# Sums of squares inside the next tile's matmuls, and a final norm with two tiles scaled ahead

## The chip, the cores and the metric

The kernel runs on one core of one Trainium2 chip, as one launch. The metric is the device time of that launch in microseconds (us), from the first to the last work of the core. The engines are called by their names in the profile: PE (TensorE, matrix products), DVE (VectorE), ACT (ScalarE), POOL (GpSimd) and SP (SyncE, which issues the DMAs here). Each engine has its own list of instructions, whose order the program fixes.

## The reference, cut to what matters

A trunk of two layers over 512 tokens of 1024 channels in fp32. Each layer has a token mixer (layer 0 a Fourier mixer, layer 1 a bidirectional retention) and a SwiGLU channel mixer. Ahead of each stands an RMS norm with a scale and a shift made from a conditioning vector; the mixer's output, times a gate, is added to x. One more norm with scale and shift ends it.

```
def rmsnorm(x, g):
    return x * lax.rsqrt(jnp.mean(x * x, axis=-1, keepdims=True) + EPS) * g

for i in range(DEPTH):
    sh1, sc1, g1, sh2, sc2, g2 = jnp.split(c_act @ w_ada[i] + b_ada[i], 6, axis=-1)
    h = modulate(rmsnorm(x, norm_mix_g[i]), sh1, sc1)
    m = fourier_mixer(h, w) if i % 2 == 0 else retention_mixer(h, ...)
    x = x + g1[:, None, :] * m
    h = modulate(rmsnorm(x, norm_ffn_g[i]), sh2, sc2)
    x = x + g2[:, None, :] * swiglu(h, w_ffn_in[i], w_ffn_out[i])
shf, scf = jnp.split(c_act @ w_ada_final + b_ada_final, 2, axis=-1)
return modulate(rmsnorm(x, final_norm_g), shf, scf)
```

So a norm needs, for each token, a sum over all 1024 channels of the x that the product ahead of it has just finished.

## The kernel before

**Layout.** x lies with channels on the partitions: 8 tiles of 128 channels by 512 tokens, kept in pairs as x[0] to x[3] (x_92 to x_95 in the program of the first layer, x_8944 to x_8950 of the second). An fp32 product is three matmuls of rounded parts (`mm3`, lines 209 to 211): high by high, high by low, low by high. `split` makes the parts: ACT casts the high part (L203), DVE takes the difference (L204).

**The four boundaries.** Four times an output projection is followed by a norm: Fourier to channel mixer 0 (the first boundary, some 75 to 130 us into the run), channel mixer 0 to retention (the second, about 447 to 500), retention to channel mixer 1 (the third, about 862 to 912), and channel mixer 1 to the final norm (the fourth, from 1203 to the end). The last piece of that projection is `out_product_last` (L599). It goes over token half t = 0, 1 (256 tokens each) and in each over the eight channel tiles j. Tile (t, j) is 12 matmuls (24 in the first boundary, which does four tiles there), then `add_gated` (L570, one DVE instruction, L571), which adds the gated product to x.

**The sums.** `Norm.sums(t, j)` (L420) turns the tile's two 128-token blocks onto the token partitions by two PE transposes (L426, called a pair here) into PSUM; they read what `add_gated` has written. After j = 3, 6 and 7 ACT squares what has been gathered and sums it (L432), and DVE scales and adds the sums (L434, L436). `SUMS = 2` says how far the sums lag: those of a tile are issued two tiles of matmuls after it, and `last_sums` (L634) does the last two.

**The rates and the modulation.** `rsqrt_steps` (L213) makes the reciprocal roots by a chain of small DVE steps (L220, L228, L231), `rate` (L445) spreads them over the partitions by two more transposes (L451), and `half` then forms the normed tiles: `modulated` (L473) is one DVE instruction (L474: x times the scale column times the rates in PSUM) and one or two ACT instructions which add the shift (L478 for the rounded high part, L479 for the fp32 one). In the second and third boundary `Quarters.half` lets DVE take the low parts by a subtraction (L508) over two tiles at a time, so an L508 needs an L478 and an L479 of both. The modulation of token half 0 (`spread(0, 0)`, `spread(0, 1)`) is emitted right after tile (1, 3), so it lies beside the products of tiles (1, 4) to (1, 7). The products that use it follow: L924 in retention and in the first channel mixer, L878 in the second one. At the end `Final.half` (L561) modulates and writes each pair of tiles with one DMA of 256 KB (L566).

**What sets the order.** The program is written as a list of steps, and a scheduler orders each engine's instructions by priority when the program is built; sums, gated adds and modulations are marked urgent (`tc.high_priority`). After that the order on each engine is fixed. Around the boundaries DVE and ACT also prepare weights: the casts and subtractions of lines 203 and 204, and sums of weight blocks (L339), all 128x1024.

Of the kernel before, what the change touches and what calls it, by code (L numbers as in the profile page):

```python
# [14 lines left out]
ALU = mybir.AluOpType  # L15
# [17 lines left out]
MASK_W = 896  # L33
LOOK = 4
LOADS = 4
SUMS = 2
URGENT = 500
PLAIN = ("00", "01", "10", "11")

# [116 lines left out]
def trunk(ctx, tc, A, where, out):  # L156
    nc = tc.nc
# [15 lines left out]
    def ps():  # L173
        return psum.tile([P, 512], F32, name="ps")

    def t2k():
        return tmp.tile([P, 512], F32, name="t2k")
# [8 lines left out]
    def tok(m):  # L186
        return slice(m * P, (m + 1) * P)

    def half(n):
        return slice(n * 512, (n + 1) * 512)  # L190
# [4 lines left out]
    def k2(t):  # L195
        return t.rearrange("p (k c) -> p k c", k=2)
# [9 lines left out]
    def mm3(o, a, b, first, last, **kw):  # L206

        (ah, al), (bh, bl) = a, b
        nc.tensor.matmul(o, ah, bh, start=first, stop=False, **kw)  # L209
        nc.tensor.matmul(o, ah, bl, start=False, stop=False, **kw)  # L210
        nc.tensor.matmul(o, al, bh, start=False, stop=last, **kw)  # L211
# [48 lines left out]
    def xt(j):  # L260

        return x[j // 2][:, half(j % 2)]
# [10 lines left out]
    def add(fn, *needs):  # L273
        program.append((needs, fn))
# [3 lines left out]
    loads, ready, mods, opening, wide, plain, homes = {}, {}, {}, set(), set(), set(), {}  # L278
# [40 lines left out]
    def use_next():  # L319
        step = steps[state["step"]]  # L320
        state["step"] += 1
        state["piece"] += len(pieces_of(step))
        issue(state["piece"] + LOADS)
        if step[0] == "ada":
            conditioning(step, loads.pop(step))
        elif len(step) == 5:
            ready[step] = combined(step)
        else:
            h, low = (k2(t) for t in high_low(loads.pop(step)))
            ready[step] = [(h[:, k, :], low[:, k, :]) for k in range(2)]  # L330
# [34 lines left out]
    def settle(key, q=ND - 1):  # L365
        if key not in shares:
            q = ND - 1
        last = at["ada", *key, q]
        while state["step"] <= last:
            use_next()  # L370
        for name, it in closing:
            if name[:2] == key and name[2] <= q:
                for _ in it:
                    pass
# [34 lines left out]
    def part(t):  # L409
        return slice(t * 256, (t + 1) * 256)  # L410
# [70 lines left out]
    class Quarters(Norm):  # L481
# [9 lines left out]
        def half(self, t, k):  # L491
            q = t4k()
            halves = [half(n) for n in range(2)]

            def held_of(tag):
# [61 lines left out]
    class Final(Norm):  # L557
        def start(self):
            pass

        def half(self, t, k):  # L561
            for j in range(4 * k, 4 * k + 4, 2):
                y = t2k()
                for i in range(2):
                    self.modulated(t, j + i, y[:, part(i)])
                nc.sync.dma_start(out=out[j * P : (j + 2) * P, part(t)].rearrange("(k p) t -> p k t", p=P), in_=k2(y))  # L566
                yield


    def add_gated(key, j, sl, o):  # L570
        nc.vector.scalar_tensor_tensor(  # L571
            out=xt(j)[:, sl], in0=o, scalar=mods[key][:, j : j + 1], in1=xt(j)[:, sl], op0=ALU.mult, op1=ALU.add
        )
# [25 lines left out]
    def out_product_last(a, names, key, following, ns=range(2)):  # L599

        w, squared = {}, []

        def act(t, n, *pieces):
            if t == 0:
                w[n] = [b for piece in pieces for b in piece]
                if n == ns[0]:
                    settle(key)
                    made["norm"] = following()
            nxt = made["norm"]
            if ns[0] == n:  # L610
                squared.extend((t, j) for j in range(4 * n))
            for c in range(4):
                j = 4 * n + c
                o = ps()[:, 0:256]
                for k, b in enumerate(w[n]):
                    first, last = k == 0, k == len(w[n]) - 1
                    b, m = [p[:, tok(c)] for p in b], [p[:, part(t)] for p in a(k)]
                    mm3(o, b, m, first, last)
                with tc.high_priority(offset=URGENT):
                    add_gated(key, j, part(t), o)  # L620
                squared.append((t, j))
                while len(squared) > SUMS:
                    nxt.sums(*squared.pop(0))
                if (t, j) == (1, 3 if ns[0] == 0 else 6):
                    nxt.rate(0)
                    nxt.spread(0, 0)
                    if ns[0] == 0:
                        nxt.spread(0, 1)

        for t in range(2):  # L630
            for n in ns:
                add(lambda *p, t=t, n=n: act(t, n, *p), *(names[n] if t == 0 else ()))

    def last_sums():  # L634
        for j in range(ND - SUMS, ND):
            made["norm"].sums(1, j)
        made["norm"].steps(1)
# [4 lines left out]
    def fourier():  # L642
# [3 lines left out]
        def front():  # L646
# [56 lines left out]
            def operand(m):  # L703
                for c in (half(n) for n in range(2)):
                    nc.scalar.mul(out=high[m][:, c], in_=xin[m][:, c], mul=rate[m])
                nc.vector.scalar_tensor_tensor(
                    out=low[m], in0=xin[m], scalar=rate[m], in1=f32(high[m]), op0=ALU.mult, op1=ALU.subtract
                )
# [627 lines left out]
```

## Time and profile before

| what | value |
| --- | --- |
| median of 3 runs | 1242.73 us (1241.94 to 1243.01) |
| the profiled execution | 1242.75 us, its span 1240.7 us |
| PE busy | 1206.7 us, 97% of the span |
| DVE busy | 1046.8 us, 84% |
| ACT busy | 580.6 us, 47% |
| POOL busy | 0.9 us |
| mean granted TensorE clock | 0.993 of full speed |

The span runs from the first to the last instruction of the profiled execution; the other 2.05 us of its time lie around it. A busy PE says that matmuls were in flight. "Idle before" in a timeline row is the time in which the engine stood ahead of that row, with what released it.

### The profile page before, as it was taken

Reading aid. Unit: us, or ns where it says so; the run is one execution under the profiler, and the core shown is the slowest. Engines: PE = TensorE matmul, PEld = TensorE weight load, DVE = VectorE, ACT = ScalarE, POOL = GpSimd, SP = SyncE. Lnnn points to the kernel's source line nnn. Section 1 sums busy time; section 2 is a strip of 40 time slices with the busy share of each in tenths; the row PEclk is TensorE's granted clock in tenths of the full one; section 3 lists DMA queues with packets and bytes.
Section 4 is the critical chain, followed back from the end, with each engine's and each line's share of the span. In section 5 each row is a group of like instructions: output and inputs, shape, how many; then the busy total and the mean of one; then the engine's idle time right before and its main releaser. Section 6 shows DMA issues by size and latency. Waiting matters only on the chain.

```text
span 1240.7 us, 20953 instructions
## 1 busy us (share of the span) xinstructions
PE 1206.7 (97%) x8456; PEld 1131.9 (91%) x8456; DVE 1046.8 (84%) x1706; ACT 580.6 (47%) x886; POOL 0.9 (0%) x8
## 2 busy tenths in 40 slices
PE   7997999999999999999999999999999999999996
PEld 6796999999999999999999999889999898999986
DVE  7998998879799769999898898965998687878855
ACT  5515754343435437545454454522765243434524
POOL 0000000000000000000000000000000000000000
PEclk9998999999999999999999999999999999999998
DMA  9785158273735721324143246862035343444302
GB/s 364 282 308 197 52 170 305 89 251 106 250 104 181 235 94 50 102 86 152 52 137 117 86 151 205 301 223 86 18 113 172 107 139 133 142 130 153 119 1 68
DMA packets 59297, 187.16 MB, mean 151 GB/s; under 512 B 5953, under 2 KB 14273, under 8 KB 59201
## 3 DMA queue, kind: packets, MB, share of 16 engines
q1 hardware_dynamic: 59200, 185.83, 44.5%
q8 instruction: 66, 1.08, 0.4%
q14 instruction: 31, 0.25, 0.1%
HBM read 178.47 MB, written 7.34 MB: 150 GB/s over the span
## 4 chain that ended last, share of the span: by engine, by line
PE 81%; DVE 10%; ACT 4%; DMA 2%; issue 2%; SPq 0%; ACTq 0%; DVEq 0%
PE ps L878 45%; PE ps L209 10%; PE ps L210 10%; PE ps L211 10%; DVE low L204 2%; PE ps L924 2%; DVE raw L391 1%; ACT t4k L479 1%; PE ps L722 1%; ACT a L478 1%; DVE raw L339 1%; DVE t4k L204 1%; DMA high<-in_w_ada 1%; DMA t4k<-in_x 1%; PE ps L426 1%
## 5 line engine op out<-in xcount | busy, mean ns | idle before, releaser
L203 ACT CAST high<-raw 128x1024 fp32r<-128x1024 f32 x259 | 271.2, 1051 | 278.0 <-PE ps L878 86.1
L204 DVE TENSOR_TENSOR low<-raw,high 128x1024 fp32r<-128x1024 f32 x259 | 315.2, 1221 | 61.4 <-ACT high L203 60.5
L878 PE MATMUL ps<-a,high 128*128 128x256 f32 x2736 | 365.6, 283 | 1.3 <-ACT a L203 1.3
L878 PEld LDWEIGHTS ps<-a,high 128*128 128x128 f32 x2736 | 346.2, 192 | 3.5 <-ACT a L203 1.5
L878 PE MATMUL ps<-a,low 128*128 128x256 f32 x1368 | 192.2, 283 | 0.0
L209 PE MATMUL ps<-t4k,high 128*128 128x512 f32 (+1 forms) x512 | 182.2, 356 | 0.0
L210 PE MATMUL ps<-t4k,high 128*128 128x512 f32 (+1 forms) x512 | 179.0, 350 | 0.0
L211 PE MATMUL ps<-t4k,low 128*128 128x512 f32 (+1 forms) x512 | 178.7, 349 | 0.0
L878 PEld LDWEIGHTS ps<-a,low 128*128 128x128 f32 x1368 | 176.5, 192 | 0.0
L391 DVE SCALAR_TENSOR_TENSOR raw<-raw,c_act 128x1024 f32<-128x1024 f32 x104 | 126.3, 1221 | 31.8 <-DMA raw<-in_w_ada 21.2
L211 PEld LDWEIGHTS ps<-t4k,low 128*128 128x128 f32 x512 | 96.6, 189 | 12.6
L878 PE MATMUL ps<-high,a 128*128 128x256 f32 x784 | 107.2, 283 | 0.8 <-ACT t2k L887 0.7
L209 PEld LDWEIGHTS ps<-t4k,high 128*128 128x128 f32 x512 | 96.7, 189 | 11.9
L210 PEld LDWEIGHTS ps<-t4k,high 128*128 128x128 f32 x512 | 96.9, 189 | 11.7
L571 DVE SCALAR_TENSOR_TENSOR x<-ps,mod,x 128x512 f32<-128x512 f32 (+1 forms) x132 | 80.8, 634 | 28.5 <-PE ps L211 28.1
L887 ACT COPY t2k<-ps 128x512 f32<-128x512 f32 x96 | 56.2, 585 | 99.9 <-PE ps L878 96.9
L878 PEld LDWEIGHTS ps<-high,a 128*128 128x128 f32 x784 | 100.5, 192 | 2.3 <-ACT t2k L887 1.2
L891 DVE TENSOR_TENSOR t2k<-t2k,ps 128x512 f32<-128x512 f32 x96 | 65.5, 683 | 13.3 <-ACT t2k L887 8.0
L339 DVE TENSOR_TENSOR raw<-raw 128x1024 f32<-128x1024 f32 x62 | 75.6, 1219 | 0.2
L203 ACT CAST t4k<-t2k 128x512 fp32r<-128x512 f32 x73 | 44.9, 619 | 33.4 <-DVE t2k L995 21.4
L204 DVE TENSOR_TENSOR t4k<-t2k,t4k 128x512 fp32r<-128x512 f32 x73 | 49.9, 686 | 8.4 <-ACT t4k L203 8.4
L209 PE MATMUL ps<-a,high 128*128 128x512 f32 (+1 forms) x160 | 56.3, 355 | 0.2 <-ACT t2k L798 0.2
(152 smaller groups left out, 1422.9 us busy)
## 6 DMA issues: line engine op xcount, KB each, us to landing
raw<-in_w_ada SPq DMA_DIRECT2D x88, 512.0 KB, 4.5
raw<-in_w_ffn_in SPq DMA_DIRECT2D x86, 512.0 KB, 4.2
raw<-in_w_ret_in SPq DMA_DIRECT2D x48, 512.0 KB, 3.3
raw<-in_w_ffn_out SPq DMA_DIRECT2D x44, 512.0 KB, 3.7
raw<-in_w_ret_out SPq DMA_DIRECT2D x16, 512.0 KB, 5.1
raw<-in_w_ada_final SPq DMA_DIRECT2D x16, 512.0 KB, 3.7
raw<-in_w_fourier_out SPq DMA_DIRECT2D x8, 512.0 KB, 7.7
z<-t2k SPq DMA_DIRECT2D x12, 256.0 KB, 3.1
```

The source lines that it names most:

```text
L203: nc.scalar.copy(out=dst_h, in_=src)
L204: nc.vector.tensor_tensor(out=dst_l, in0=src, in1=f32(dst_h), op=ALU.subtract)
L209: nc.tensor.matmul(o, ah, bh, start=first, stop=False, **kw)
L210: nc.tensor.matmul(o, ah, bl, start=False, stop=False, **kw)
L211: nc.tensor.matmul(o, al, bh, start=False, stop=last, **kw)
L339: eng.tensor_tensor(out=dst, in0=p, in1=q, op=ALU.subtract)
L391: nc.vector.scalar_tensor_tensor(out=t, in0=t, scalar=1.0, in1=c_act, op0=ALU.mult, op1=ALU.mult, accum_out=v[:, q : q + 1])
L571: nc.vector.scalar_tensor_tensor(out=xt(j)[:, sl], in0=o, scalar=mods[key][:, j : j + 1], in1=xt(j)[:, sl], op0=ALU.mult, op1=ALU.add)
L878: nc.tensor.matmul(o[:, j * 256 : (j + 1) * 256], a, b, start=tag in "127" and n == m == j == k == 0, stop=n == 1 and k == 3, skip_group_c ...
L887: nc.scalar.copy(out=t, in_=o)
L891: nc.vector.tensor_tensor(out=t, in0=t, in1=self.z if tag == "5" else o, op=ALU.add)
L924: nc.tensor.matmul(o[:, j * 256 : (j + 1) * 256], a, b, start=k == n == m == j == c == 0, stop=k == n == 1 and c == 3, skip_group_check=True,)
```

## The change

`SUMS` goes from 2 to 1, and the sums are no longer issued after a tile's gated add: they are issued inside the matmuls of the next tile, after 9 of its 12 (15 of 24 in the first boundary). `last_sums` then has one tile left. At the final norm ACT multiplies tiles 0 and 1 of token half 1 by their scale columns as soon as they are added (`scaled`); when the rates are there, ACT copies them from PSUM to SBUF, GpSimd multiplies the two tiles by them, and DVE adds the shifts. The other six tiles go as before, and the output goes in the order 2, 4, 6, 0.

```
-SUMS = 2
+SUMS = 1
...
+        def scaled(self, j):
+
+            if j == 0:
+                settle(self.key[0])
+                self.ahead = t2k()
+            nc.scalar.mul(out=self.ahead[:, part(j)], in_=xt(j)[:, part(1)], mul=mods[self.key[0]][:, j : j + 1])
+
         def half(self, t, k):
-            for j in range(4 * k, 4 * k + 4, 2):
-                y = t2k()
+            if t and k == 0:
+                r, y = t2k()[:, 0:256], self.ahead
+                nc.scalar.copy(out=r, in_=self.r[t])
                 for i in range(2):
-                    self.modulated(t, j + i, y[:, part(i)])
+                    nc.gpsimd.tensor_tensor(out=y[:, part(i)], in0=y[:, part(i)], in1=r, op=ALU.mult)
+            for j in ((0, 2), (4, 6))[k] if t == 0 else ((2, 4), (6, 0))[k]:
+                if (t, j) == (1, 0):
+                    y = self.ahead
+                    for i in range(2):
+                        sh = mods[self.key[1]][:, i : i + 1]
+                        nc.vector.tensor_scalar(out=y[:, part(i)], in0=y[:, part(i)], scalar1=sh, scalar2=None, op0=ALU.add)
+                else:
+                    y = t2k()
+                    for i in range(2):
+                        self.modulated(t, j + i, y[:, part(i)])
...
                 for k, b in enumerate(w[n]):
+                    if k == len(w[n]) // 2 + 1:
+                        while len(squared) > SUMS - 1:
+                            nxt.sums(*squared.pop(0))
...
                     add_gated(key, j, part(t), o)
+                if t == 1 and j < 2 and isinstance(nxt, Final):
+                    nxt.scaled(j)
                 squared.append((t, j))
-                while len(squared) > SUMS:
-                    nxt.sums(*squared.pop(0))
```

Line numbers of the changed kernel: `add_gated` L589 (was L571), the products L945 and L899 (L924 and L878); in the lines up to 479, and for L508, the numbers stay.

**Place 1: PE at the second boundary, the sums of tile (1, 4).** Rows are operation, result and operands; x2_94 holds tiles 4 and 5, ps_4848 and ps_4834 are the products of tiles (1, 6) and (1, 5), ps_4866 and ps_4852 those of the tiles after them. Before:

```order
L210 MATMUL ps_4848<-t4k_4364,high_4485 128x256
L211 MATMUL ps_4848<-t4k_4363,low_4486 128x256
L426 MATMUL ps_4862<-ident_96,x2_94 128x128
L426 MATMUL ps_4864<-ident_96,x2_94 128x128
L209 MATMUL ps_4866<-t4k_4132,high_4451 128x256
L210 MATMUL ps_4866<-t4k_4133,high_4451 128x256
```

and with the change:

```order
L210 MATMUL ps_4834<-t4k_4364,high_4485 128x256
L211 MATMUL ps_4834<-t4k_4363,low_4486 128x256
L426 MATMUL ps_4844<-ident_96,x2_94 128x128
L426 MATMUL ps_4846<-ident_96,x2_94 128x128
L209 MATMUL ps_4852<-t4k_4132,high_4451 128x256
L210 MATMUL ps_4852<-t4k_4133,high_4451 128x256
```

The pair of tile (1, 4) stood after tile (1, 6); it now stands after tile (1, 5), 12 matmuls earlier. (The one of tile (1, 3) moves likewise, from after tile (1, 5) to one matmul into it.)

**Place 2: DVE at the second boundary.** x_93 holds tiles 2 and 3, x_94 tiles 4 and 5; L474 writes the modulated tiles, and L508 takes low parts from them and from what ACT has made of them. Before:

```order
L571 SCALAR_TENSOR_TENSOR x_93<-ps,mod_1608,x_93 128x256
L204 TENSOR_TENSOR low<-raw,high 128x1024
L474 SCALAR_TENSOR_TENSOR t4k<-x_92,mod_2186,ps 128x256 x2
L474 SCALAR_TENSOR_TENSOR t4k<-x_93,mod_2186,ps 128x256 x2
L474 SCALAR_TENSOR_TENSOR t4k<-x_94,mod_2186,ps 128x256 x2
L474 SCALAR_TENSOR_TENSOR t4k<-x_95,mod_2186,ps 128x256 x2
L571 SCALAR_TENSOR_TENSOR x_94<-ps,mod_1608,x_94 128x256
L508 TENSOR_TENSOR a_4778<-t4k,a_4777 128x512
L508 TENSOR_TENSOR a_4795<-t4k,a_4794 128x512
L571 SCALAR_TENSOR_TENSOR x_94<-ps,mod_1608,x_94 128x256
```

and with the change:

```order
L204 TENSOR_TENSOR low<-raw,high 128x1024
L589 SCALAR_TENSOR_TENSOR x_93<-ps,mod_1608,x_93 128x256
L474 SCALAR_TENSOR_TENSOR t4k<-x_92,mod_2186,ps 128x256 x2
L474 SCALAR_TENSOR_TENSOR t4k<-x_93,mod_2186,ps 128x256 x2
L474 SCALAR_TENSOR_TENSOR t4k<-x_94,mod_2186,ps 128x256 x2
L474 SCALAR_TENSOR_TENSOR t4k<-x_95,mod_2186,ps 128x256 x2
L434 TENSOR_SCALAR ss_4823<-ss_4823 128x1
L508 TENSOR_TENSOR a_4780<-t4k,a_4779 128x512
L508 TENSOR_TENSOR a_4797<-t4k,a_4796 128x512
L589 SCALAR_TENSOR_TENSOR x_94<-ps,mod_1608,x_94 128x256 x2
L204 TENSOR_TENSOR low<-raw,high 128x1024
L339 TENSOR_TENSOR raw<-raw 128x1024
```

The gated add of tile (1, 4), the first of x_94, stood right after the eight L474; it now stands after them, an L434 and two L508. The third boundary has the same rows in the same order.

**Place 3: ACT at the second boundary.** L203 casts weights, L478 and L479 add the shifts, and L432 squares four turned tiles (j = 0 to 3) of one token block. Before:

```order
L203 CAST high<-raw 128x1024 x2
L478 ACTIVATE a_4777<-t4k,mod_2741 128x256 x2
L479 ACTIVATE t4k<-t4k,mod_2741 128x256 x2
L478 ACTIVATE a_4777<-t4k,mod_2741 128x256
L478 ACTIVATE a_4794<-t4k,mod_2741 128x256 x2
L479 ACTIVATE t4k<-t4k,mod_2741 128x256 x2
L478 ACTIVATE a_4794<-t4k,mod_2741 128x256
L479 ACTIVATE t4k<-t4k,mod_2741 128x256 x2
L478 ACTIVATE a_4794<-t4k,mod_2741 128x256
L478 ACTIVATE a_4777<-t4k,mod_2741 128x256
L479 ACTIVATE t4k<-t4k,mod_2741 128x256 x2
L432 ACTIVATE ps,ss_4841<-ps 128x512
```

and with the change:

```order
L203 CAST high<-raw 128x1024 x2
L432 ACTIVATE ps,ss_4823<-ps 128x512
L478 ACTIVATE a_4779<-t4k,mod_2741 128x256 x2
L479 ACTIVATE t4k<-t4k,mod_2741 128x256 x2
L478 ACTIVATE a_4796<-t4k,mod_2741 128x256 x2
L479 ACTIVATE t4k<-t4k,mod_2741 128x256 x2
L478 ACTIVATE a_4779<-t4k,mod_2741 128x256
L478 ACTIVATE a_4796<-t4k,mod_2741 128x256
L479 ACTIVATE t4k<-t4k,mod_2741 128x256 x2
L478 ACTIVATE a_4796<-t4k,mod_2741 128x256
L478 ACTIVATE a_4779<-t4k,mod_2741 128x256
L432 ACTIVATE ps,ss_4827<-ps 128x512
```

The first square of the gathered tiles now stands ahead of the L478 and L479 of the modulation, the second one inside them.

## Rows read from the trace of the kernel before

**Rows 1.** The page: busy time by engine, and the chain that ended last by engine
```profile
PE 1206.7 (97%) x8456; PEld 1131.9 (91%) x8456; DVE 1046.8 (84%) x1706; ACT 580.6 (47%) x886; POOL 0.9 (0%) x8
...
PE 81%; DVE 10%; ACT 4%; DMA 2%; issue 2%; SPq 0%; ACTq 0%; DVEq 0%
```

**Rows 2.** PE's waits, whole run: what waited, for what, total us, times, longest
```profile
PE ps L924 <- ACT t4k L478: 4.3, 2, 3.2
...
PE ps L924 <- DVE a L204: 3.3, 1, 3.3
PE ps L451 <- DVE rs_y L231: 3.1, 3, 2.4
PE ps L924 <- ACT a L478: 3.1, 2, 2.7
...
PE ps L426 <- DVE x L571: 1.9, 4, 0.8
...
PE ps L878 <- ACT a L203: 1.3, 1, 1.3
PE ps L878 <- ACT t2k L887: 0.7, 1, 0.7
```

**Rows 3.** PE's timeline, second boundary: start, duration, instruction, count, idle before
```profile
457.25 0.38 PE L426 MATMUL ps<-ident,x 128*128 128x128 f32 x2
...
458.91 0.38 PE L426 MATMUL ps<-ident,x 128*128 128x128 f32 x2
459.13 0.38 PE L451 MATMUL ps<-ident,rs_y 128*128 128x128 f32 x2
...
464.31 0.44 PE L426 MATMUL ps<-ident,x 128*128 128x128 f32 x2
```

**Rows 4.** DVE's timeline, second boundary
```profile
459.11 0.48 DVE L571 SCALAR_TENSOR_TENSOR x<-ps,mod,x 128x256 f32<-128x256 f32 x1 [0.37 <-PE ps L211]
459.51 1.22 DVE L204 TENSOR_TENSOR low<-raw,high 128x1024 fp32r<-128x1024 f32 x1
460.64 3.21 DVE L474 SCALAR_TENSOR_TENSOR t4k<-x,mod,ps 128x256 f32<-128x256 f32 x8
463.78 0.47 DVE L571 SCALAR_TENSOR_TENSOR x<-ps,mod,x 128x256 f32<-128x256 f32 x1
464.18 1.41 DVE L508 TENSOR_TENSOR a<-t4k,a 128x512 fp32r<-128x512 f32 x2
```

**Rows 5.** ACT's timeline, second boundary
```profile
461.15 0.91 ACT L478 ACTIVATE a<-t4k,mod 128x256 fp32r<-128x256 f32 x2 [0.89 <-DVE t4k L474]
...
467.57 0.57 ACT L432 ACTIVATE ps<-ps 128x512 f32<-128x512 f32 x1
468.08 0.18 ACT L432 ACTIVATION_READ_ACCUMULATOR ps<-ps 128x1 f32 x1
```

**Rows 6.** DVE's timeline, third boundary
```profile
874.84 3.22 DVE L474 SCALAR_TENSOR_TENSOR t4k<-x,mod,ps 128x256 f32<-128x256 f32 x8
877.97 0.48 DVE L571 SCALAR_TENSOR_TENSOR x<-ps,mod,x 128x256 f32<-128x256 f32 x1
878.37 1.41 DVE L508 TENSOR_TENSOR a<-t4k,a 128x512 fp32r<-128x512 f32 x2
```

**Rows 7.** DVE's timeline, fourth boundary
```profile
1222.94 3.22 DVE L474 SCALAR_TENSOR_TENSOR t2k<-x,mod,ps 128x256 f32<-128x256 f32 x8
1226.08 0.87 DVE L571 SCALAR_TENSOR_TENSOR x<-ps,mod,x 128x256 f32<-128x256 f32 x2
...
1233.63 3.23 DVE L474 SCALAR_TENSOR_TENSOR t2k<-x,mod,ps 128x256 f32<-128x256 f32 x8 [0.57 <-PE ps L451]
```

**Rows 8.** ACT's timeline, the last row of the run
```profile
1234.15 3.30 ACT L479 ACTIVATE t2k<-t2k,mod 128x256 f32<-128x256 f32 x8 [2.86 <-DVE t2k L474]
```

**Rows 9.** Windows: stretch, its length, busy time and count by engine, granted clock, DMA share, GB/s
```profile
107.00:110.00 3.00, 2.77 (x13) 2.77 (x14) 3.00 (x11) 0.00 (x0) 0.00 (x0) 0.50 0.84 276
...
1236.00:1239.00 3.00, 0.00 (x0) 0.00 (x0) 0.86 (x3) 1.45 (x4) 0.00 (x0) 0.50 0.99 329
```

**Rows 10.** POOL's timeline: its one instruction of arithmetic
```profile
1.01 0.29 POOL masks.py:199 TENSOR_SCALAR_AFFINE_SELECT ident<-ident 128x128 f32<-128x128 f32 x1
```

## The prediction

> **What bounds the kernel now.** I read the page's busy times and its chain of waits first: PE is busy for 97% of the span and carries 81% of the chain, DVE 10% [rows 1]. So a microsecond in which PE stands is a microsecond of the run, unless PE would have stood later anyway. Then PE's own waits, to see what it can still win [rows 2]: the sums wait for gated adds four times, 1.9 us in all; the rates wait for their chain of small DVE steps three times, 3.1 us with a longest of 2.4, so 0.7 in the two others (0.4 in the second boundary, 0.3 in the third); products wait for modulated tiles, 4.3 us with a longest of 3.2 (that one in the first boundary, the other 1.1 in the second); 1.3 and 0.7 us stand for L878, in the third and second boundary. The long ones of L924, 3.3, 3.2 and 2.7, are all in the first boundary. Last the timelines of the three engines at the second boundary, side by side [rows 3 to 5]. The reader is to see there how narrowly the sums of tile (1, 4) fit: DVE adds that tile at 463.78, right behind eight L474, and PE turns it at 464.31, with some 0.2 us of standing (three periods of 1.66 after the rates at 459.13 would be 464.1).
>
> **The unit of the sum.** From pair to pair PE takes 458.91 - 457.25 = 1.66 us, of which a pair takes 459.13 - 458.91 = 0.22; the 12 matmuls are 1.44, so 0.12 each [rows 3].
>
> **Second boundary: the new stall.** *PE.* Two more pairs stand before the end of tile (1, 3), which moves from 458.91 to 459.3. With the rates' pair (0.22), tile (1, 4) (1.44) and one matmul PE is at the sums of (1, 3) at 461.1. Their add stands behind an L204 now (Place 2; 1.13 us from row to row) and so ends near 461.35 [rows 4]. A pair and eleven matmuls later, at 462.9, PE wants the sums of (1, 4), 1.4 us earlier than before.
>
> *DVE.* It is later with that add, not earlier. The eight L474 run from 461.3 to 464.4 (3.14 from row to row). The first L508 follows. The second reads tiles 4 and 5, so it needs the first four L478 and four L479. ACT makes 16 of these in 467.57 - 461.15 = 6.4 us, 0.40 each [rows 5], and begins them behind the first square (Place 3): the pair ends at 461.6, the square and its reading take 0.75 to 462.4, and eight times 0.40 gives 465.6. L508 (0.66) and the gated add (0.47) [rows 4] end at 466.75. **PE stands from 462.9 to 466.75, 3.85 us.** Without any delay by ACT it would still be 464.4 + 1.3 + 0.4 = 466.1, 3.2 us.
>
> *A second hold.* From there PE needs 21 matmuls and two pairs to the sums of (1, 6), 3.0 us, to 469.7. But the add of (1, 6) now stands behind the add of (1, 5) (0.4), an L204 and an L339 (1.13 each), and two L508 (1.3): 466.7 + 4.0 + 0.4 = 471.1. The clock adds little to that: after the 3.3 us stall of the first boundary PE's granted clock was 0.50 (its 1.2 GHz level) for some 3 us [rows 9]; half of 3.0 us of matmuls in that time would bring PE there at 471.2. I take a further 1.5 us, so that PE is 5.4 us behind at equal work.
>
> *Given back.* The waits that stood behind: 0.4 for the rates and 1.1 for the modulated tiles [rows 2], since sums (1, 7) are done early against their use and DVE and ACT went on meanwhile. Net **+3.9**. Bounds: 3.2 without the ACT delay and without the second hold, less 1.5 and less the 0.7 of L878 too, +1.0; and 5.4 with nothing given back.
>
> **Third boundary.** Same places in the code, same order, same times to a tenth (eight L474 at 874.84, add at 877.97, L508 at 878.37) [rows 6]. The same 5.4. Given back are the 0.3 for the rates and half of the 1.3 for a weight cast [rows 2], which DVE and ACT prepare while PE stands: **+4.5**, bounds 1.6 and 5.4.
>
> **Fourth boundary.** There is no L508 here. PE wants the sums of (1, 4) at 1226.0 (15 matmuls after those of (1, 3)). The add stands, as before, behind the eight L474, which start some 0.45 later than the 1222.94 of now and end at 1226.55 [rows 7]; add to 1227.05: 1.0 us. The last add's sums come 1.4 later, but the wide square of token block 0 is then done beside the last tile, so the rates come about 1.0 later. *The tail.* Now eight L474 and eight L479 end it, 0.41 each for ACT [rows 7, 8]. With the change ACT first copies the rates (0.4, the price of an L479) beside the first L474, then does six L479: it ends 0.4 earlier counted from the rates. POOL's two products are not in any row. From below 0.40 (an L474 of this size), from above 0.58, twice the 0.29 of POOL's only arithmetic, which has half the elements [rows 10]; at 0.58 both are done 1.6 us after the rates, while DVE needs 2.4 for its six L474 before it comes to the shifts, so POOL has a cover of 0.8 us and costs nothing; past that, each further microsecond costs one. What ACT wins meets the transfers: DMA is 99% busy at 329 GB/s in the tail [rows 9], so 256 KB take 0.8 us, and the last two are now issued within 0.3. I give back 0 of the 0.4 and add 0.1: **+1.1**, bounds 0 and +2.
>
> **First boundary.** The adds come earlier, so the 3.3 us wait for L204 shrinks by up to 1.4; but the 2.7 and 3.2 behind it [rows 2] hang on DVE, which is full there (3.00 of 3.00 us) [rows 9], and the modulation is not earlier by more than some 0.5. **-0.3**, bounds -1 and +0.8.
>
> **Sum.** -0.3 + 3.9 + 4.5 + 1.1 = **+9.2** on the profiled execution's 1242.75, so 1252.0. The median of the runs, 1242.73, is the same. Bounds added up: +1.6 and +13.6.
>
> **Rivals.**
>
> *1. The stalls are short and are paid back (no change).* Suppose DVE reached the add of (1, 4) as soon as its data allow: rates spread at 459.13, L474 some 0.5 later, no L204 between, no ACT delay, eight L474 (3.1), two L508 (1.3) and the add (0.5). It would end at 464.5, 1.6 us of standing. Less 1.5 + 0.7 in the second boundary, less 0.3 + 1.3 in the third, with 0 at the end and -0.3 at the start: -0.3 - 0.6 + 0 = -0.9, 1241.9. For it: PE is the chain elsewhere, so DVE and ACT get ahead while it stands. Against: the order on DVE is fixed, with L204 and L508 in the way.
>
> *2. Faster.* The adds are in time, no sum waits, and the rates' waits and the late products (0.7, 1.1 and 1.3) go, with 0.3 at the start and 0.8 from the two L479 in the tail: 4.2 us less, 1238.5. It decides at 462.9: it needs the add of (1, 4) done by then. Against it: eight L474 and the add behind rates that are spread at 459.13 [rows 3, 4], some 0.5 + 3.1 + 0.5, cannot end before 463.2, even with nothing between them.
>
> *3. POOL is late.* Its first product comes later than its bound from rows. It decides at the cover of 0.8 us worked out above; past that the tail ends with products, shifts and one transfer, and each microsecond costs one. With a first product as late as ACT's whole last row, 3.3 us [rows 8], that is 2.5 over the forecast, 1254.5. For and against: AFFINE_SELECT, POOL's only arithmetic so far, shows 0.29 us [rows 10]; it is another operation, at the start. The Trainium skill, GPSIMD Engine Reference, section 2.1 (Instruction dispatch), says that the first call to a freshly loaded GpSimd kernel pays about 6 us for its code, with no instruction to show for it; by that figure the tail would be, as an estimate, 5 us longer, and the run 1257. No row here shows it.
>
> *4. Clock.* If each 3.85 us stall costs the next 3 us at half clock in full, and the second hold does not cover it, 1.5 more at each of two places: 1255.
>
> **Chances.** Forecast 0.75, rival 1 0.09, rival 2 0.07, rival 3 0.05, rival 4 0.04. The lower half of the forecast (no second hold: 1.5 less twice, 1249; more given back, down to 1245) and both upper rivals go into the range: 1244.5 to 1256. It leaves out rivals 1 and 2 and a little above. This kernel's measurement can tell about 0.2%, 2.5 us: faster 0.07, within 0.2% 0.10, slower 0.83.
>
> **What would show it.** *Right:* in PE's waits, the line of the sums waiting for the gated add (L426 for L589) goes from 1.9 us to about 10, with 3.8 us once each in the second and third boundary at the pair of (1, 4), and some 1.5 at the pair of (1, 6); on DVE, the second L508 idle for ACT's L479 ahead of that add; the waits of L945 for L478 and of L451 for the rates gone from the second boundary. In the tail, six L479, two POOL products beside the L474, and DMA close to full. *Wrong:* a wait of L426 under 2 us at these pairs (rival 1), none (rival 2), a gap on POOL ahead of its first product (rival 3), or PE's clock at 0.50 well past the second hold (rival 4).

## The result, and the profile after

The changed kernel takes **1251.24 us** (median of 6 runs, 1250.26 to 1252.38) against 1242.68 for the kernel before on the same chips: 8.6 us more by the medians, and a ratio of 1.0074 (95% interval 1.0064 to 1.0085). One of the six executions of the kernel before took 2398.04 us and is left out of the ratio. The forecast was 1252.0. The profiled execution took 1251.28 us, with a span of 1249.2 against 1240.7.

The page after, busy time and chain, beside that of before in [rows 1]:

```profile
PE 1207.8 (97%) x8456; PEld 1132.9 (91%) x8456; DVE 1045.3 (84%) x1706; ACT 582.1 (47%) x887; POOL 2.3 (0%) x10
...
PE 92%; DVE 3%; DMA 2%; ACT 2%; issue 0%; SPq 0%; ACTq 0%; DVEq 0%
```

No engine is busier by more than 1.5 us. So most of the 8.5 us of span are standing and not work (a part is PE working at a lower clock, see the third boundary below), and busy shares would not have shown them. PE's waits tell where, beside [rows 2]:

```profile
PE ps L426 <- DVE x L589: 11.2, 7, 3.7
...
PE ps L451 <- DVE rs_y L231: 3.6, 3, 2.1
PE ps L945 <- ACT t4k L478: 3.2, 1, 3.2
...
PE ps L945 <- DVE a L204: 2.5, 1, 2.5
PE ps L945 <- ACT a L478: 1.9, 3, 1.4
...
PE ps L899 <- ACT a L203: 1.2, 1, 1.2
```

The sums' wait for the gated add went from 1.9 to 11.2 us: 1.1 in the first boundary, 5.0 in the second, 3.7 in the third and 1.5 in the fourth. Of the waits for modulated tiles the 1.1 of the second boundary is gone, and PE no longer waits for the rates there.

PE at the second boundary, beside [rows 3]: the pairs of tiles (1, 3), (1, 4) and (1, 6).

```profile
460.82 0.44 PE L426 MATMUL ps<-ident,x 128*128 128x128 f32 x2
...
466.24 0.44 PE L426 MATMUL ps<-ident,x 128*128 128x128 f32 x2 [3.67 <-DVE x L589]
...
470.68 0.44 PE L426 MATMUL ps<-ident,x 128*128 128x128 f32 x2 [1.30 <-DVE x L589]
```

DVE there, beside [rows 4], from the eight L474 to the add of tile (1, 6), and ACT, beside [rows 5]:

```profile
460.68 3.21 DVE L474 SCALAR_TENSOR_TENSOR t4k<-x,mod,ps 128x256 f32<-128x256 f32 x8
...
463.88 0.68 DVE L508 TENSOR_TENSOR a<-t4k,a 128x512 fp32r<-128x512 f32 x1
465.09 0.69 DVE L508 TENSOR_TENSOR a<-t4k,a 128x512 fp32r<-128x512 f32 x1 [0.53 <-ACT t4k L479]
465.70 0.87 DVE L589 SCALAR_TENSOR_TENSOR x<-ps,mod,x 128x256 f32<-128x256 f32 x2
...
468.94 1.28 DVE L508 TENSOR_TENSOR a<-t4k,a 128x512 fp32r<-128x512 f32 x2
470.15 0.48 DVE L589 SCALAR_TENSOR_TENSOR x<-ps,mod,x 128x256 f32<-128x256 f32 x1
```

```profile
461.19 0.58 ACT L432 ACTIVATE ps<-ps 128x512 f32<-128x512 f32 x1 [1.12 <-PE ps L426]
...
461.77 0.90 ACT L478 ACTIVATE a<-t4k,mod 128x256 fp32r<-128x256 f32 x2
```

Read the three together. PE comes to the sums of (1, 4) at 466.24 - 3.67 = 462.6 and stands until DVE's add at 465.70 has written. DVE is busy with the L474 up to 463.8, then with the first L508, and then idle for 0.53 us ahead of the second L508, for ACT, which began the modulation only after a square. The second hold, 1.30 us, is PE's wait for the add of (1, 6), which starts at 470.15.

The third boundary: PE at the pairs of (1, 4), (1, 5) and (1, 6); DVE from the L474 to the add of (1, 6); and two of the microseconds between (length, PE's busy time and matmuls, granted clock, DMA share, GB/s):

```profile
883.29 0.44 PE L426 MATMUL ps<-ident,x 128*128 128x128 f32 x2 [3.67 <-DVE x L589]
...
884.98 0.63 PE L426 MATMUL ps<-ident,x 128*128 128x128 f32 x2
...
887.81 0.38 PE L426 MATMUL ps<-ident,x 128*128 128x128 f32 x2
```

```profile
877.74 3.21 DVE L474 SCALAR_TENSOR_TENSOR t4k<-x,mod,ps 128x256 f32<-128x256 f32 x8
...
882.14 0.69 DVE L508 TENSOR_TENSOR a<-t4k,a 128x512 fp32r<-128x512 f32 x1 [0.54 <-ACT t4k L479]
882.75 0.87 DVE L589 SCALAR_TENSOR_TENSOR x<-ps,mod,x 128x256 f32<-128x256 f32 x2
...
887.07 0.48 DVE L589 SCALAR_TENSOR_TENSOR x<-ps,mod,x 128x256 f32<-128x256 f32 x1
```

```profile
885.00:886.00 1.00, 1.00 (x6) 0.50 0.36 49
886.00:887.00 1.00, 1.00 (x7) 0.50 0.73 274
```

The stall is the same 3.67 us, for the same reason, but there is no second hold: here the granted clock fell to 0.50 (1.2 GHz) after the stall, so that PE came to (1, 6) at 887.81, behind the add (887.07, 0.48 long). From the pair of (1, 4) to that of (1, 6) PE takes 887.81 - 883.29 = 4.52 us. In the second boundary the same stretch takes 470.68 - 466.24 = 4.44 us, of which 1.30 is the wait, so 3.14 us at the full clock. So the clock cost 1.38 us here, where the second boundary lost 1.30 to waiting.

The tail, beside [rows 7, 8, 10], in the order DVE, ACT, POOL:

```profile
1242.08 2.44 DVE L474 SCALAR_TENSOR_TENSOR t2k<-x,mod,ps 128x256 f32<-128x256 f32 x6 [0.82 <-ACT t2k L571]
1244.43 0.61 DVE L579 TENSOR_SCALAR t2k<-t2k,mod 128x256 f32<-128x256 f32 x2
```

```profile
1241.67 0.37 ACT L571 COPY t2k<-ps 128x256 f32<-128x256 f32 x1 [2.20 <-PE ps L451]
1242.60 2.52 ACT L479 ACTIVATE t2k<-t2k,mod 128x256 f32<-128x256 f32 x6 [0.55 <-DVE t2k L474]
```

```profile
1242.13 1.41 POOL L573 TENSOR_TENSOR t2k<-t2k 128x256 f32<-128x256 f32 x2 [1196.86 <-ACT t2k L571]
```

ACT ends 1242.60 + 2.52 - 1241.26 = 3.86 us after the rates' chain (its last L231 ends at 1241.26) instead of 4.38 (1237.45 - 1233.07). The transfers behind it use that up. The windows of the last transfers, before and then after (length, ACT busy, clock, DMA share, GB/s):

```profile
1235.75:1236.00 0.25, 0.25 (x2) 0.50 0.08 25
...
1239.00:1239.25 0.25, 0.00 (x0) 0.50 0.67 226
```

```profile
1244.25:1244.50 0.25, 0.25 (x2) 0.50 0.23 78
...
1247.50:1247.75 0.25, 0.00 (x0) 0.50 0.43 140
```

In both the transfers fill some 3.2 us from first to last. So the start of the first one decides, and that is 0.25 us later counted from the rates: the first L474 stands 0.82 us, for ACT's copy, where it stood 0.57 for PE [rows 7].

To see which boundary cost what, I cut each profile at two long runs of products, one after the first boundary (450 of L878) and one after the third (424). In the chain of before and of after:

```profile
140.86 54.00 PE ps L878 x450
...
907.11 51.14 PE ps L878 x424
```

```profile
140.25 54.00 PE ps L899 x450
...
914.15 51.14 PE ps L899 x424
```

A third cut, at a run of 13 products (525.17 before, 527.78 after), parts the second boundary from the third. In us:

| kernel | first pair of sums to 450 | 450 to 13 | 13 to 424 | 424 to the end |
| --- | --- | --- | --- | --- |
| before | 64.57 | 384.31 | 381.94 | 333.6 |
| changed | 63.70 | 387.53 | 386.37 | 335.1 |
| changed, second profile | 64.71 | 387.53 | 387.42 | 335.0 |
| sums_only | 64.63 | 388.54 | 386.33 | 334.6 |
| final_only | 64.48 | 384.31 | 381.69 | 333.9 |
| adds_first | 64.23 | 384.66 | 381.55 | 333.6 |
| square_late | 63.15 | 385.60 | 385.09 | 334.6 |
| lag2in | 62.97 | 384.71 | 382.55 | 333.5 |
| half0_rate2 | 64.45 | 384.04 | 380.97 | 333.6 |
| best1 | 64.10 | 384.05 | 380.98 | 333.5 |
| best2 | 64.68 | 384.05 | 380.95 | 333.4 |

In the first profile of the changed kernel the second boundary costs 3.2 us more than before, the third 4.4, the fourth with the tail 1.5, and the first 0.9 less; the sums of the first boundary began 0.26 later. Where code is the same and the clock did the same, the columns agree within 0.3, but for the first one, of which more below.

### The profile page after: what moved, and what is told of

Read it like the earlier page. It is cut to its first block, busy times and chain, and to the rows that moved or that the text cites. A ratio compares the mean times of both kernels' runs of the same rounds, so it can differ in the third digit from the quotient of the medians.

```text
span 1249.2 us, 20955 instructions
## 1 busy us (share of the span) xinstructions
PE 1207.8 (97%) x8456; PEld 1132.9 (91%) x8456; DVE 1045.3 (84%) x1706; ACT 582.1 (47%) x887; POOL 2.3 (0%) x10
## 4 chain that ended last, share of the span: by engine, by line
PE 92%; DVE 3%; DMA 2%; ACT 2%; issue 0%; SPq 0%; ACTq 0%; DVEq 0%
PE ps L899 52%; PE ps L209 11%; PE ps L210 11%; PE ps L211 11%; PE ps L945 3%; PE ps L426 1%; PE ps L743 1%; DMA high<-in_w_ada 1%; DVE low L204 1%; DMA t4k<-in_x 1%; DVE raw L391 1%; PE ps L1174 1%; ACT high L203 0%; PE ps L813 0%; DMA keep<-x 0%
## 5 line engine op out<-in xcount | busy, mean ns | idle before, releaser
L203 ACT CAST high<-raw 128x1024 fp32r<-128x1024 f32 x259 | 271.5, 1051 | 287.8 <-PE ps L899 96.4
L204 DVE TENSOR_TENSOR low<-raw,high 128x1024 fp32r<-128x1024 f32 x259 | 315.4, 1221 | 62.2 <-ACT high L203 61.1
L899 PE MATMUL ps<-a,high 128*128 128x256 f32 x2736 | 365.7, 284 | 1.2 <-ACT a L203 1.2
L899 PEld LDWEIGHTS ps<-a,high 128*128 128x128 f32 x2736 | 346.2, 192 | 3.3 <-ACT a L203 1.4
L899 PE MATMUL ps<-a,low 128*128 128x256 f32 x1368 | 192.2, 283 | 0.0
L899 PEld LDWEIGHTS ps<-a,low 128*128 128x128 f32 x1368 | 176.5, 192 | 0.0
L391 DVE SCALAR_TENSOR_TENSOR raw<-raw,c_act 128x1024 f32<-128x1024 f32 x104 | 126.4, 1221 | 32.6 <-DMA raw<-in_w_ada 22.4
L899 PE MATMUL ps<-high,a 128*128 128x256 f32 x784 | 106.8, 283 | 0.7 <-ACT t2k L908 0.7
L589 DVE SCALAR_TENSOR_TENSOR x<-ps,mod,x 128x512 f32<-128x512 f32 (+1 forms) x132 | 80.9, 633 | 30.1 <-PE ps L211 30.1
L908 ACT COPY t2k<-ps 128x512 f32<-128x512 f32 x96 | 56.3, 586 | 103.4 <-PE ps L899 100.5
L899 PEld LDWEIGHTS ps<-high,a 128*128 128x128 f32 x784 | 100.4, 192 | 1.8 <-ACT t2k L908 0.9
L203 ACT CAST t4k<-t2k 128x512 fp32r<-128x512 f32 x73 | 44.9, 618 | 27.6 <-DVE t2k L1016 16.4
L204 DVE TENSOR_TENSOR t4k<-t2k,t4k 128x512 fp32r<-128x512 f32 x73 | 49.9, 686 | 8.6 <-ACT t4k L203 8.5
```

The source lines that it names most:

```text
L203: nc.scalar.copy(out=dst_h, in_=src)
L204: nc.vector.tensor_tensor(out=dst_l, in0=src, in1=f32(dst_h), op=ALU.subtract)
L391: nc.vector.scalar_tensor_tensor(out=t, in0=t, scalar=1.0, in1=c_act, op0=ALU.mult, op1=ALU.mult, accum_out=v[:, q : q + 1])
L589: nc.vector.scalar_tensor_tensor(out=xt(j)[:, sl], in0=o, scalar=mods[key][:, j : j + 1], in1=xt(j)[:, sl], op0=ALU.mult, op1=ALU.add)
L899: nc.tensor.matmul(o[:, j * 256 : (j + 1) * 256], a, b, start=tag in "127" and n == m == j == k == 0, stop=n == 1 and k == 3, skip_group_c ...
L908: nc.scalar.copy(out=t, in_=o)
```

## The experiments

The theory (A) is the prediction's: PE stands at sums whose gated add is held on DVE by what the scheduler has put ahead of it. Each kernel was timed beside the kernel before; a ratio is to that, with its 95% interval.

**sums_only**: the changed kernel with the `Final` of before and no call of `scaled`.

> The sums as in the changed kernel, the final norm as before. Theory A (PE stands at sums whose gated add is held on DVE behind L474 and L508): the whole loss stays, 1251 us (1250.3 to 1251.8), with PE's wait of L426 for the gated add at 3.7 us once each in the second and third boundary. Rival B (the new tail, with ACT's copy and POOL, costs a good part): 1249 or less.

1250.78 us, ratio 1.0068 (1.0055 to 1.0081). PE's waits have the 3.67 twice again. In this profile the clock fell at the second boundary too, which cost 4.2 us here. Its pair of (1, 4) and a window behind it:

```profile
466.75 0.69 PE L426 MATMUL ps<-ident,x 128*128 128x128 f32 x2 [3.67 <-DVE x L571]
```

```profile
467.00:468.00 1.00, 1.00 (x6) 0.50 0.18 57
```

So the loss is the sums', not the tail's.

**final_only**: the kernel before with the changed `Final` and the calls of `scaled`.

> The final norm as in the changed kernel, the sums as before. Theory A: 1242.7 us (1242.1 to 1243.3), the sums' waits of before (1.9 us in all). Rival B: 1244 or more. In the tail ACT should be done some 0.4 us earlier counted from the end of the rates' chain, and the last transfer no earlier.

1242.52 us, ratio 1.0002 (0.9993 to 1.0010). Rival B falls: this half of the change is worth nothing that can be measured, either way. Its first L474 again waits for the copy:

```profile
1233.60 2.44 DVE L474 SCALAR_TENSOR_TENSOR t2k<-x,mod,ps 128x256 f32<-128x256 f32 x6 [0.82 <-ACT t2k L571]
```

**adds_first**: sums_only, and

```
-                with tc.high_priority(offset=URGENT):
+                with tc.high_priority(offset=4 * URGENT):
                     add_gated(key, j, part(t), o)
```

> As sums_only, but the gated adds are urgent four times as much, which puts those of tiles (1, 4) to (1, 6) between the L474 on DVE; PE's sums keep their early places. Theory A: the stalls go, 1243 us (1242 to 1245), L426's waits for the gated add under 2.5 us in all. Rival C (transposes inside a tile's matmuls cost PE time wherever DVE is): 1250 to 1251.

1242.25 us, ratio 1.0000 (0.9991 to 1.0008). Its wait of the sums for the gated add, whole run, and DVE at the second boundary:

```profile
PE ps L426 <- DVE x L571: 1.1, 2, 0.7
```

```profile
460.76 0.47 DVE L474 SCALAR_TENSOR_TENSOR t4k<-x,mod,ps 128x256 f32<-128x256 f32 x1
461.14 0.48 DVE L571 SCALAR_TENSOR_TENSOR x<-ps,mod,x 128x256 f32<-128x256 f32 x1
461.54 1.25 DVE L474 SCALAR_TENSOR_TENSOR t4k<-x,mod,ps 128x256 f32<-128x256 f32 x3
```

This is the run that decides. PE wants the sums as early as in the changed kernel (those of (1, 4) three matmuls earlier still), the adds stand between the L474 on DVE, and the 8.5 us are gone. (ACT's second wide square comes earlier with them, so the adds are not the only thing that moved.) Rival C falls: the place of the transposes inside a tile's matmuls costs nothing that can be measured. Nor is this kernel faster than the one before: with the stalls repaired, the early sums win nothing.

**square_late**: sums_only, and the square of tile (1, 3) not urgent.

```
-                with tc.high_priority(offset=URGENT):
+                with tc.high_priority(offset=URGENT if (t, j) != (1, 3) else 0):
                     nc.scalar.activation(out=o[:, cols], in_=o[:, cols], func=AF.Square, accum_out=ss)
```

> As sums_only, but the first wide square of token half 1 is not urgent. On ACT its place stays ahead of the modulation; on DVE the gated add of tile (1, 4) comes between the first and the second L508 (which waits for ACT), no longer behind both. Theory A: the stall at the sums of (1, 4) in the second and third boundary falls from 3.7 to 2.4 us each, the second hold at (1, 6) goes too, so 1246 us (1245 to 1247.5). Rival D (the stall is set by the eight L474 alone, and what stands after them is beside the point): 3.7 us each as now, 1250.8.

1246.86 us, ratio 1.0044 (1.0031 to 1.0056). DVE and PE at the second boundary:

```profile
463.12 0.68 DVE L508 TENSOR_TENSOR a<-t4k,a 128x512 fp32r<-128x512 f32 x1
463.72 0.47 DVE L571 SCALAR_TENSOR_TENSOR x<-ps,mod,x 128x256 f32<-128x256 f32 x1
464.39 0.69 DVE L508 TENSOR_TENSOR a<-t4k,a 128x512 fp32r<-128x512 f32 x1 [0.20 <-ACT t4k L479]
```

```profile
464.25 0.44 PE L426 MATMUL ps<-ident,x 128*128 128x128 f32 x2 [2.38 <-DVE x L571]
```

With one L508 and its wait for ACT less ahead of the add, the stall is 2.38 us instead of 3.67, as forecast, so rival D falls. The second hold is gone. The second boundary now costs 1.3, the third 3.2, since the clock fell there (0.50 in 881 to 882) and no second hold covered what that cost.

**lag2in**: sums_only with `SUMS = 2`, so that the sums are inside a tile's matmuls, but of the tile before the last.

> Sums inside a tile's matmuls as in the change, but those of the tile before the last one (lag as before, three matmuls earlier than before); final norm as before. Theory A: PE wants the sums of (1, 4) when the add is nearly there, a wait under 0.7 us each, 1242.3 us (1241.7 to 1243.3). Rival C (the place inside a tile itself costs): 1250.

1242.46 us, ratio 1.0005 (0.9996 to 1.0015). PE's pair of (1, 4):

```profile
463.97 0.44 PE L426 MATMUL ps<-ident,x 128*128 128x128 f32 x2 [0.93 <-DVE x L571]
```

The time is as expected; the wait was to be under 0.7 and is 0.93, once each in the second and third boundary. The table has +0.4 and +0.6 for the two boundaries; the timed runs can't tell that from nothing. The clock stayed at 1.00 behind them.

**half0_rate2**: sums of token half 0 early, those of half 1 as before, rates and modulation one tile earlier.

```
-                        while len(squared) > SUMS - 1:
+                        while squared and squared[0][0] == 0:
                             nxt.sums(*squared.pop(0))
...
                 squared.append((t, j))
+                while t == 1 and len(squared) > 2:
+                    nxt.sums(*squared.pop(0))
-                if (t, j) == (1, 3 if ns[0] == 0 else 6):
+                if (t, j) == (1, 2 if ns[0] == 0 else 6):
```

> Sums of token half 0 inside the next tile's matmuls, those of half 1 two tiles late as before, and the rates and modulation of half 0 emitted after tile (1, 2), not (1, 3); final norm as before. Theory A: no stall at the sums (under 2 us in all), and L474 comes 1.6 us earlier, so the products' waits behind it shrink: 1241 us (1239.5 to 1242.5). Rival C: half of the loss stays, 1246.

1241.14 us, ratio 0.9986 (0.9977 to 0.9995). DVE's L474 at the second boundary start 2.8 us earlier than before [rows 4], ahead of the L204, and no sums wait there:

```profile
457.82 3.23 DVE L474 SCALAR_TENSOR_TENSOR t4k<-x,mod,ps 128x256 f32<-128x256 f32 x8
```

The second boundary gains 0.3 and the third 1.0. This kernel beats the one before by 0.14%, which is within what I called no change. The expectation named the wrong source for it: the waits of products for modulated tiles and weight casts did not shrink (1.1 and 0.7 us in the second boundary, 1.2 in the third, against 1.1, 0.7 and 1.3). What went is the 0.2 of standing at the sums of (1, 4), in both boundaries, and the 0.3 for the rates in the third; where the rest was won is open.

**best1**: half0_rate2 with the sums of both halves early in the first boundary. **best2**: best1 with the first and last pair of output tiles written as two DMAs of 128 KB each.

```
-                        while squared and squared[0][0] == 0:
+                        while squared and (ns[0] or squared[0][0] == 0):
...
-                while t == 1 and len(squared) > 2:
+                while not ns[0] and t == 1 and len(squared) > 2:
```

> As half0_rate2 in the second to fourth boundary, and in the first the sums of both halves inside the next tile's matmuls, as in the change. Theory A: the changed kernel's gain of some 0.9 us in the first boundary is added to that of half0_rate2: 1240.3 us (1239.5 to 1241.2). If the first boundary's gain was an accident of the load order: 1241.1.

> As best1, and at the end the first and the last pair of output tiles are written by two DMAs of 128 KB each. If the transfers bound the tail, it begins 0.4 us earlier and ends with a smaller one: 0.3 to 0.8 us less than best1. If SP's issuing bounds it (two more issues), as much or 0.4 us more.

1240.80 us, ratio 0.9989 (0.9980 to 0.9998), and 1240.51, 0.9988 (0.9979 to 0.9996). Neither is apart from half0_rate2. So I ran these three again on one chip, with the changed kernel, whose first boundary was in question.

> The changed kernel once more, for the stretch of the first boundary (from PE's first pair of sums to the 450 products after it): 63.70 us in its profile, 64.57 in that of before. If the 0.87 us is the change's, it stays within 0.2; if it hangs on when the early loads land, it differs by over 0.4. The time: 1251.2 us (1250.3 to 1252.3), with 3.7 us at the sums of (1, 4) in the second and third boundary again.

> half0_rate2 once more, beside best1 and best2 on one chip: 1241.1 us, 0.1% under before. Second and third boundary as in its first profile, -0.3 and -1.0 us against before; first boundary 64.45 us then, now within 0.2 if it is the kernel's, over 0.4 off if it is the loads'.

> best1 once more: if the first boundary's early sums give something, 0.3 us or more under half0_rate2 on the same chip; if not, within 0.2 of it.

> best2 once more: if the split transfers give something, 0.2 us or more under best1 on the same chip; if not, within 0.2 of it.

The changed kernel: 1252.35 us, ratio 1.0079 (1.0065 to 1.0093), 0.05 us above the expected range, with the two 3.67 again. half0_rate2 1240.80 (0.9990, 0.9981 to 0.9999), best1 1240.84 (0.9992, 0.9984 to 1.0001), best2 1240.63 (0.9986, 0.9977 to 0.9995): one time, within their intervals. In the first boundary the changed kernel took 64.71 us this time, 1.0 more than in its first profile; half0_rate2 64.97 against 64.45, best1 64.64 against 64.10, best2 64.33 against 64.68. So the 0.9 us that the first boundary seemed to win is scatter between executions of one program (on different chips), and best1's early sums win nothing that was measured. What sets that scatter is open. The loads of in_w_ada, for which DVE's L391 waits in that stretch, do not explain it: that wait is 1.1 us in both profiles of the changed kernel. PE's wait for the rates there differs, 1.4 and 2.7 us. best2's split is inconclusive: its medians are 0.3 and 0.2 us under best1, which just reaches what was expected of it, but inside both intervals.

## Why the prediction was right, point by point

- **PE is the chain, standing counts.** Right: busy times hardly moved, waits did, and the span followed them. The kernel that takes the waits away (adds_first) takes the loss away.
- **Second boundary, stall.** Forecast 3.85 us from 462.9 to 466.75; measured 3.67 from 462.6 to 466.24. Its parts held: L474 to 463.81 (forecast 464.4), a wait for ACT's L479 ahead of the second L508, the square ahead of the L478. The whole stretch came 0.3 to 0.6 earlier, mostly because this run reached the boundary earlier. In sums_only, which reached it when the kernel before did, the L474 start at 461.20 (forecast 461.3) and PE stands from 463.1 to 466.75.
- **Second hold.** Forecast 1.5; measured 1.30 in the second boundary, and 1.38 as lost clock in the third.
- **Given back.** The 0.4 and 1.1 us in the second boundary are gone, as forecast. Standing of 3.67 + 1.30, less these and the 0.2 of before, is 3.2, which is the table's +3.2 (forecast +3.9: the stall 0.2 and the hold 0.2 shorter, and the small wait of before not taken off). The 0.7 for L887 (L908 now) stayed, as forecast.
- **Third boundary.** Forecast +4.5, measured +4.4 and +5.5 in two profiles. One part was wrong: half of the 1.3 for a weight cast was to come back, and the wait is still 1.2. The sum of the first profile came out all the same because other parts were smaller: 3.67 and 1.38, less the 0.3 for the rates, 0.1 of the cast and the 0.2 of standing that the kernel before has at these sums too, is 4.45.
- **Fourth boundary.** Forecast +1.1, measured +1.5, of which sums_only has 1.0. The term that was mis-sized is the copy of the rates: I laid it beside the first L474, but the L474 wait for it (0.82 against 0.57). And POOL's product takes 0.70 us (1.41 for two), over my upper bound of 0.58, which scaled a POOL row of another operation by elements. It still lay in its cover: done at 1243.54, the shifts start at 1244.43.
- **First boundary.** Forecast -0.3, measured -0.9 in the first profile and +0.1 in the second. The wait for L204 shrank, as forecast (3.3 to 2.5 and 2.4), but waits for the rates came in, which the forecast did not have (none before, 1.4 and 2.7 now). The net can't be told from scatter.
- **Rivals.** 1 and 2 fell with the waits of 3.67. 3 fell: POOL's first product starts 0.09 us after ACT's copy ends (1241.67 + 0.37). The price of some 6 us for the first call to a freshly loaded kernel, which the Trainium skill gives (GPSIMD Engine Reference, section 2.1, Instruction dispatch), does not show here; whether these products are such a call, no row tells. 4 is half true: in three profiles (changed kernel twice, sums_only) the clock fell at five of six such stalls, but then no 1.30 us of hold followed: PE, slowed by the clock, came to (1, 6) when the add was done. So the places cost +3.2 to +5.5 us, and not 3.9 and 4.5 with 1.5 more on each. Hence 1251 to 1252, not 1255.
- **Luck.** That the sum, +9.2, came within a microsecond of the measured +8.6 is in part luck. In the first profile the second boundary came out 0.7 lower and the first 0.6 lower (by scatter), the fourth 0.4 higher. And when the clock fell at a stall differed between executions, which alone moved the third boundary by 1.05 us (+4.43 and +5.48).

## What to carry to other kernels

Moving a consumer earlier helps only if its producer has a place as early in the order of its own engine. Before such a move, list what the producer's engine has ahead of it, and what that waits for on a third engine; here eight modulation steps, two low-part subtractions and their wait for ACT made 3.7 us of standing at two places out of a move that was to save time. If the consumer's engine is the bound, repair the producer's order first (adds_first), or leave the lag where nothing needs the result yet (half0_rate2). And ask first what the move can win: here, with the stalls gone, it won nothing (adds_first), and half0_rate2 won 0.14%.

## What the runs showed of the hardware

**The clock after a stall differs from run to run.** After the same stall of 3.67 us at the same place (second boundary) the granted clock stayed at 1.00 in the first profile of the changed kernel, and was at 0.50 in its second profile; two windows of the second:

```profile
467.00:468.00 1.00, 1.00 (x6) 0.50 0.09 16
468.00:469.00 1.00, 1.00 (x6) 0.50 0.94 381
```

In square_late 2.38 us left it at 1.00 in the second boundary and at 0.50 in the third; in lag2in 0.93 us left it at 1.00 twice.

**DVE's first read of the rates in PSUM began only when ACT's copy of them was done.** DVE stands for 0.82 us ahead of the first L474, with ACT's copy as its releaser, in the changed kernel and in final_only, although the L474 need nothing that the copy writes; it starts 0.04 us after the copy ends (1241.67 + 0.37 to 1242.08). Whether the chip or the built program orders the two reads was not tried.
